# Two buffers for the gate and value rows of an up projection, four instead of five for the left weight parts

## The chip, the cores and the metric

The kernel runs on one core of a Trainium2 chip. The metric is device time in microseconds (us), the median over the runs shown. Times inside the kernel come from one profiled execution.

## What is computed

One decoder layer for 2048 tokens of 1024 features: a mixing block (attention and a recurrent part), and behind it a gated feed-forward block with a causal convolution of width 3. The change is in the feed-forward block:

```python
def conv_gated_ffn(h, w_up, conv_w, conv_b, w_down):
    u = h @ w_up                                   # 1024 -> 2 * 4096
    u_pad = jnp.pad(u, ((0, 0), (CONV_WIDTH - 1, 0), (0, 0)))
    u = conv_b + sum(conv_w[j] * u_pad[:, j:j + S] for j in range(CONV_WIDTH))
    gate, val = jnp.split(u, 2, axis=-1)
    return (jax.nn.gelu(gate, approximate=True) * val) @ w_down

x = x + rms_norm(f, norm_ffn_post[l])              # f: what conv_gated_ffn returns
```

## The kernel before

Phase A projects the input, phase B runs attention, the recurrence and the output projection, and phase D (`phase_d`) is the feed-forward block. All products are float32: each operand is split into a high part (rounded, by a cast on ScalarE, line 40) and a low part (the difference, on VectorE, line 41), and three matmuls replace one (high-high, low-high, high-low).

Both projections of phase D use a Strassen-like scheme with seven products instead of eight. In the up projection the sequence is taken in two halves of 1024 tokens, and in each half there are 32 units; unit n has 128 gate rows and 128 value rows. A unit has seven products j, each of 12 matmuls of 128x512 (line 250) into a bank of PSUM. For each product the weights are combined on GpSimd (lines 218, 219, 224, 227) out of the raw tile `wr`, which two transfers fill (line 205), and split into `wh` and `wl` by `wprep`. The parts of j = 0, 1, 4, 5 come from the left pool, those of j = 2, 3, 6 from the right pool of four buffers. The split activations `hh` and `hl` stay for a whole half.

`product(n, j)` runs the matmuls, and `post(n, j)` what follows. For j = 0, 2, 3 ScalarE copies the bank to `sum` (line 280). For j = 1 a new `ug` tile is taken, two columns of the last half are copied into it (`utile`, line 256), and VectorE adds the `sum` and a bank into its first half (line 276); for j = 4 the second half is added, and `conv` makes the gate: ScalarE does the first tap (line 266), VectorE the other two (lines 267 and 268), and ScalarE the GELU (line 286). For j = 5 a new `uv` tile is taken and its second half added (line 276), and product j = 6 goes on in the same bank `a`; for j = 6 ScalarE copies the bank to `uv` (line 290), the value's convolution follows, and VectorE multiplies gate and value (line 293). Every second unit also writes sums and differences of the results (`sa`, lines 305 to 308), on GpSimd and VectorE. In the first half line 264 keeps two columns of `u` in `halo`.

The units overlap in pairs. In the steady order the slots of seven products are: j=0 of n, j=5 of n-1, j=1 of n, j=4 of n-1, j=2 of n, j=6 of n-1, j=3 of n. `wprep` stands five slots (`LEAD`) ahead of its product in the program. The program's order is the order of priority; the library's planner then orders each engine's instructions by a model of their time, and gives out the buffers of a pool as they come free. Each engine runs its instructions in the planned order. Tiles of a pool that have the same name share the pool's `bufs` buffers.

The down projection takes over the `up_` pool for one constant row (`gpost`).

Of the kernel before, what the change touches and what calls it, by code (L numbers as in the profile page):

```python
# [101 lines left out]
def phase_d(ctx, tc, x1, h2t, w_up, cw, halo, w_down, g_post, mhalf, out, hq, act, td):  # L102
# [8 lines left out]
    with ExitStack() as es:  # L111


        pool = lambda name, bufs=1, side="left": es.enter_context(tc.tile_pool(name=name, bufs=bufs, side=side))
        hrp, wrp, wsp = pool("dr", 2), pool("drw", 2), pool("dsw", 3)
        wps = {"left": pool("dwl", 5)}
        bps = {i: pool(f"d{i}", side="left" if i < 8 else "right") for i in range(14)}
        wps["right"] = pool("dwr", 4, "right")
        up_, ep = pool("du", side="right"), pool("de", side="right")
        pss = [es.enter_context(tc.tile_pool(name=f"dp{i}", bufs=1, space=PSUM)) for i in range(8)]  # L120
        w0c, w1c, w2c, bc = (cw[:, i * 64:(i + 1) * 64] for i in range(4))

# [1042 lines left out]
def hybrid_layer(ctx, tc, a, c, out):  # L1165
# [25 lines left out]
    phase_b(ctx, tc, s, x, a["w_out"][0], a["norm_mix_post"], a["norm_ffn_pre"], a["sinks"], c["tri"], ident, mhalf, gc, line, x1, h2t, hq[0],  # L1191
            cw, a["conv_w"][0], a["conv_b"][0])
    phase_d(ctx, tc, x1, h2t, a["w_ffn_up"][0], cw, halo, a["w_ffn_down"][0], a["norm_ffn_post"],
            mhalf, out[0], hq, act, td)

# [38 lines left out]
```

## Time and profile before

| | |
|---|---|
| median of 3 runs | 3162.61 us (3157.29 to 3166.73) |
| the profiled execution | 3158.45 us, span 3156.6 us |
| TensorE matmul busy | 3043.6 us, 96% of the span |
| TensorE weight load busy | 2458.3 us, 78% |
| VectorE busy | 2302.4 us, 73% |
| ScalarE busy | 1448.5 us, 46% |
| GpSimd busy | 1098.2 us, 35% |

The profile names engines PE (TensorE matmul), PEld (its weight load, which overlaps PE), DVE (VectorE), ACT (ScalarE), POOL (GpSimd) and SP (the queue that issues the transfers). The matmuls are pipelined and their ends are modelled, so the distance of their starts says more than their durations. Idle time stands ahead of the instruction that ended it, with the instruction that released it.

### The profile page before, as it was taken

Reading aid. Unit: us, or ns where it says so; the run is one execution under the profiler, and the core shown is the slowest. Engines: PE = TensorE matmul, PEld = TensorE weight load, DVE = VectorE, ACT = ScalarE, POOL = GpSimd, SP = SyncE. Lnnn points to the kernel's source line nnn. Section 1 sums busy time; section 2 is a strip of 40 time slices with the busy share of each in tenths; the row PEclk is TensorE's granted clock in tenths of the full one; section 3 lists DMA queues with packets and bytes.
Section 4 is the critical chain, followed back from the end, with each engine's and each line's share of the span. In section 5 each row is a group of like instructions: output and inputs, shape, how many; then the busy total and the mean of one; then the engine's idle time right before and its main releaser. Section 6 shows DMA issues by size and latency. Waiting matters only on the chain.

```text
span 3156.6 us, 46475 instructions
## 1 busy us (share of the span) xinstructions
PE 3043.6 (96%) x17897; PEld 2458.3 (78%) x17897; DVE 2302.4 (73%) x3170; ACT 1448.5 (46%) x2438; POOL 1098.2 (35%) x903
## 2 busy tenths in 40 slices
PE   8999999979999998899999999999999999999997
PEld 6788888767777776778787877888887788888786
DVE  6778787766767666999998998888888843334555
ACT  6465756344444445444444445444444432333332
POOL 2212112123323523554444443444444420003642
PEclk9999999969999999999999999999999999999999
DMA  5736363653445635433333343333333474446764
GB/s 162 195 123 187 114 170 104 186 169 108 130 123 161 201 92 196 153 118 101 101 101 101 115 150 123 100 100 100 100 103 101 160 267 151 149 140 227 279 214 167
DMA packets 523762, 461.14 MB, mean 146 GB/s; under 512 B 117306, under 2 KB 405396, under 8 KB 522516
## 3 DMA queue, kind: packets, MB, share of 16 engines
q1 hardware_dynamic: 523540, 458.17, 45.4%
q8 instruction: 140, 2.29, 0.3%
q14 instruction: 82, 0.67, 0.1%
HBM read 316.00 MB, written 142.09 MB: 145 GB/s over the span
## 4 chain that ended last, share of the span: by engine, by line
PE 27%; DVE 18%; DMA 7%; issue 5%; ACT 3%; POOL 0%; SPq 0%; DVEq 0%; POOLq 0%; ACTq 0%
PE b L398 18%; PE b L250 9%; DVE wl L41 7%; DMA wr<-in_w_ffn_up 6%; DVE yg L293 3%; DVE yv L268 2%; ACT yg L266 2%; DVE uv L256 1%; ACT wh L40 1%; DVE ug L276 1%; DVE uv L276 1%; DVE sa L307 0%; DVE sa L306 0%; DVE do L41 0%; DVE yg L267 0%
## 5 line engine op out<-in xcount | busy, mean ns | idle before, releaser
L250 PE MATMUL b<-hh,wh 128*128 128x512 f32 x1792 | 708.9, 396 | 48.0 <-DVE uv L276 33.9
L250 PE MATMUL b<-hh,wl 128*128 128x512 f32 x1792 | 704.8, 394 | 0.5 <-DVE wl L41 0.5
L250 PE MATMUL b<-hl,wh 128*128 128x512 f32 x1792 | 704.7, 393 | 0.2 <-DVE hl L41 0.2
L398 PE MATMUL b<-do 128*128 128x512 f32 x2688 | 613.0, 390 | 5.0 <-DVE do L41 5.0
L398 PEld LDWEIGHTS b<-do 128*128 128x128 f32 x2688 | 506.1, 188 | 111.4 <-DVE do L41 5.9
L41 DVE TENSOR_TENSOR wl<-wr,wh 128x512 fp32r<-128x512 f32 (+1 forms) x400 | 435.1, 1093 | 54.6 <-ACT wh L40 53.3
L250 PEld LDWEIGHTS b<-hh,wh 128*128 128x128 f32 x1792 | 340.3, 190 | 136.7 <-DVE uv L276 47.8
L250 PEld LDWEIGHTS b<-hh,wl 128*128 128x128 f32 x1792 | 339.9, 190 | 74.4 <-DVE wl L41 1.2
L250 PEld LDWEIGHTS b<-hl,wh 128*128 128x128 f32 x1792 | 340.1, 190 | 72.1 <-DVE hl L41 0.6
L41 DVE TENSOR_TENSOR do<-ar,do 128x2048 fp32r<-128x2048 f32 x56 | 138.2, 2467 | 311.4 <-ACT do L40 311.4
L40 ACT CAST wh<-wr 128x512 fp32r<-128x512 f32 (+1 forms) x400 | 274.8, 703 | 172.2 <-PE pj L30 103.5
L218 POOL TENSOR_TENSOR s<-wr 128x512 f32<-128x512 f32 x64 | 131.5, 2054 | 518.1 <-DMA wr<-in_w_ffn_up 518.1
L40 ACT CAST do<-ar 128x2048 fp32r<-128x2048 f32 x56 | 107.1, 1912 | 363.3 <-PE b L398 346.9
L30 PE MATMUL pj<-hh,wh 128*128 128x512 f32 x640 | 256.9, 403 | 4.7 <-ACT hh L40 3.1
L30 PE MATMUL pj<-hh,wl 128*128 128x512 f32 x640 | 255.3, 400 | 0.0
L30 PE MATMUL pj<-hl,wh 128*128 128x512 f32 x640 | 255.0, 400 | 0.0
L161 POOL TENSOR_TENSOR br<-br 128x1024 f32<-128x1024 f32 x32 | 94.9, 2964 | 459.2 <-DMA br<-d_td 358.3
L266 ACT ACTIVATE yg<-ug,cw 128x1024 f32<-128x1024 f32 x64 | 79.7, 1245 | 320.7 <-DVE ug L276 319.0
L40 ACT CAST wh<-s 128x512 fp32r<-128x512 f32 x128 | 79.5, 622 | 189.8 <-POOL s L219 186.4
L30 PEld LDWEIGHTS pj<-hh,wh 128*128 128x128 f32 x640 | 123.0, 192 | 33.3 <-ACT hh L40 3.5
L30 PEld LDWEIGHTS pj<-hl,wh 128*128 128x128 f32 x640 | 122.7, 192 | 26.7
L30 PEld LDWEIGHTS pj<-hh,wl 128*128 128x128 f32 x640 | 122.6, 192 | 26.7
(280 smaller groups left out, 5399.5 us busy)
## 6 DMA issues: line engine op xcount, KB each, us to landing
wr<-in_w_ffn_up SPq DMA_DIRECT2D x128, 512.0 KB
ar<-d_act SPq DMA_DIRECT2D x112, 512.0 KB
br<-in_w_ffn_down SPq DMA_DIRECT2D x72, 512.0 KB
wr<-in_w_in SPq DMA_DIRECT2D x64, 512.0 KB
d_act<-sa SPq DMA_DIRECT2D x32, 1024.0 KB
d_act<-yg SPq DMA_DIRECT2D x32, 512.0 KB
xt<-in_x SPq DMA_DIRECT2D x28, 512.0 KB
d_bk<-bk SPq DMA_DIRECT2D x16, 512.0 KB
```

Of the source, the lines that this page charges most:

```text
L30: nc.tensor.matmul(out=out, lhsT=a, rhs=b, start=first and i == 0 and j == 0, stop=last and i == n - 1 and j == 2)
L40: nc.scalar.copy(out=hi, in_=raw)
L41: nc.vector.tensor_tensor(out=lo, in0=raw, in1=hi, op=ALU.subtract)
L161: nc.gpsimd.tensor_tensor(out=br[:, 0], in0=br[:, 0], in1=br[:, 1], op=ALU.subtract)
L218: tt(out=r[1], in0=t[:, 2], in1=t[:, 3], op=ALU.add)
L250: nc.tensor.matmul(out=o, lhsT=a[:, k, :], rhs=b[:, k, :], start=j in (0, 1, 3) and k == 0 and i == 0, stop=k == 3 and i == 2, skip_group_ ...
L256: nc.vector.tensor_copy(out=u[:, 0:2], in_=halo[:, col, :])
L266: nc.scalar.activation(out=y, in_=u[:, 2:], func=AF.Identity, scale=w2c[:, col:col + 1], bias=bc[:, col:col + 1])
L268: nc.vector.scalar_tensor_tensor(out=y, in0=u[:, 0:SB], scalar=w0c[:, col:col + 1], in1=y, op0=ALU.mult, op1=ALU.add)
L276: nc.vector.tensor_tensor(out=out, in0=x, in1=y, op=ALU.add)
L293: nc.vector.tensor_tensor(out=y, in0=y, in1=yv, op=ALU.mult)
L398: nc.tensor.matmul(out=bks[n], lhsT=x[:, 2 * h + m, a], rhs=b[:, y], start=k == 0 and p not in CHAIN and m == 0 and j == 0, stop=last and ...
```

## The change

The pool of `ug` and `uv` gets two buffers for each of the two tiles. The pool of the left `wh` and `wl` has four of each instead of five.

```diff
         hrp, wrp, wsp = pool("dr", 2), pool("drw", 2), pool("dsw", 3)
-        wps = {"left": pool("dwl", 5)}
+        wps = {"left": pool("dwl", 4)}
         bps = {i: pool(f"d{i}", side="left" if i < 8 else "right") for i in range(14)}
         wps["right"] = pool("dwr", 4, "right")
-        up_, ep = pool("du", side="right"), pool("de", side="right")
+        up_, ep = pool("du", 2, "right"), pool("de", side="right")
```

A left buffer pair takes 2 x 2 KB of each partition, a `ug` or `uv` buffer 4104 bytes.

## Rows read from the trace of the kernel before

**Rows 1.** Line 250's instructions (min/median/max ns); busy us of PE PEld DVE ACT POOL, clock

```profile
L250 PE MATMUL b<-hh,wh x1792: 387/389/794, 1203.4 to 2524.3; 128*128 128x512 f32 x200
1300.00:1400.00 100.00, 88.24 (x364) 70.45 (x363) 88.83 (x92) 39.14 (x60) 54.82 (x32) 0.95 0.41 141
1700.00:1800.00 100.00, 99.06 (x435) 81.06 (x434) 90.78 (x103) 47.23 (x73) 47.33 (x26) 1.00 0.32 106
```

**Rows 2.** Waits of TensorE, 1220 to 2500 us: total us, times, longest

```profile
PE b L250 <- DVE uv L276: 32.6, 32, 4.0
PE b L250 <- ACT sum L280: 5.0, 3, 2.3
```

**Rows 3.** Timeline of TensorE: start us, us, instruction [idle before <-releaser]

```profile
1307.62 0.79 PE L250 MATMUL b<-hh,wh 128*128 128x512 f32 x1 [3.95 <-DVE uv L276]
...
1500.05 0.39 PE L250 MATMUL b<-hh,wh 128*128 128x512 f32 x1
...
1507.98 0.39 PE L250 MATMUL b<-hh,wl 128*128 128x512 f32 x1
...
1531.64 0.50 PE L250 MATMUL b<-hh,wh 128*128 128x512 f32 x1 [0.73 <-DVE uv L276]
...
1958.33 0.50 PE L250 MATMUL b<-hh,wh 128*128 128x512 f32 x1 [3.70 <-DVE uv L276]
```

**Rows 4.** Timeline of VectorE, two units of the steady part

```profile
1489.90 1.25 DVE L256 COPY uv<-halo 128x2 f32<-128x2 f32 x1
...
1514.24 0.68 DVE L276 TENSOR_TENSOR ug<-sum,b 128x512 f32<-128x512 f32 x1
...
1516.23 1.28 DVE L267 SCALAR_TENSOR_TENSOR yg<-ug,cw,yg 128x1024 f32<-128x1024 f32 x1 [0.73 <-ACT yg L266]
...
1519.35 0.17 DVE L256 COPY ug<-halo 128x2 f32<-128x2 f32 x1
1519.43 0.68 DVE L276 TENSOR_TENSOR ug<-sum,b 128x512 f32<-128x512 f32 x1
...
1521.58 1.28 DVE L267 SCALAR_TENSOR_TENSOR yv<-uv,cw,yv 128x1024 f32<-128x1024 f32 x1 [0.87 <-ACT yv L266]
1523.41 0.69 DVE L41 TENSOR_TENSOR wl<-wr,wh 128x512 fp32r<-128x512 f32 x1 [0.55 <-ACT wh L40]
...
1525.21 1.78 DVE L41 TENSOR_TENSOR wl<-wr,wh 128x512 fp32r<-128x512 f32 x1
1526.91 2.31 DVE L293 TENSOR_TENSOR yg<-yg,yv 128x1024 f32<-128x1024 f32 x1
1529.14 1.25 DVE L256 COPY uv<-halo 128x2 f32<-128x2 f32 x1
...
1530.91 0.68 DVE L276 TENSOR_TENSOR uv<-sum,b 128x512 f32<-128x512 f32 x1
...
1533.27 0.67 DVE L276 TENSOR_TENSOR ug<-sum,b 128x512 f32<-128x512 f32 x1
```

**Rows 5.** Chain of work that ended last, 1490 to 1570: start us, us, what

```profile
1518.15 4.59 DMA wr<-in_w_ffn_up
1522.76 0.63 ACT wh L40
```

**Rows 6.** Instructions of lines 276, 293, 256 and 41: ns min/median/max, first and last start

```profile
L276 DVE TENSOR_TENSOR ug<-sum,b x128: 671/677/687, 1224.7 to 2524.9; 128x512 f32<-128x512 f32 x128
L293 DVE TENSOR_TENSOR yg<-yg,yv x64: 1208/2306/2315, 1285.0 to 2532.1; 128x1024 f32<-128x1024 f32 x64
L256 DVE COPY uv<-halo x64: 152/1256/1269, 1221.1 to 2521.3; 128x2 f32<-128x2 f32 x64
L41 DVE TENSOR_TENSOR wl<-s,wh x128: 675/681/1784, 1222.1 to 2493.4; 128x512 fp32r<-128x512 f32 x128
```

**Rows 7.** Timeline of GpSimd in the same stretch

```profile
1528.10 2.27 POOL L224 TENSOR_TENSOR wr<-wr 128x512 f32<-128x512 f32 x1
1532.81 1.69 POOL L227 TENSOR_TENSOR wr<-wr,s 128x512 f32<-128x512 f32 x1 [0.69 <-DVE halo L264]
```

## The prediction

> **What bounds the kernel now.** I read the busy shares by stretch first, since the change touches only the up projection (its matmuls run from 1203.4 to 2524.3 us) and buffers that it uses. In its steady part TensorE is busy 99 per cent at the full granted clock and VectorE 91; near the start TensorE falls to 88 [rows 1]. Second the waits of TensorE in this stage: nearly all of its idle time, 32.6 us in 32 stalls, ends with the add that writes `uv` (L276); no stall of any size waits for a weight part [rows 2]. Third its timeline: matmuls start every 0.2266 us (35 steps from 1500.05 to 1507.98), so the 168 matmuls of two units (a unit is one n, seven products of 12) need 38.07 us. One stall per two units is shown, 0.73 us of idle at 1531.64 [rows 3]; there are 27 of at most 1.5 us on this add, and five larger ones, the first of 3.95 us and the last of 3.70, 14.8 us together, around the start of each half of the sequence [rows 3].
>
> Why there: product j=6 goes into the bank that the add of j=5 still has to read, so TensorE cannot start it before that add. The add sits far back in VectorE's queue. Two units of VectorE, from one `uv` halo copy at 1489.90 to the same copy two units later at 1529.14, take 39.24 us [rows 4], 1.17 us more than TensorE needs. So **the loop that sets the pace is VectorE together with ScalarE**, by 3 per cent, although VectorE is not busy all the time: it waits for ScalarE 0.73 us before the first tap of the gate's convolution, 0.87 us before that of the value's, and in every other unit 0.55 us for a weight cast [rows 4]. The chain of waits tells the same and names one more member: the transfer of the next raw weights (4.59 us), the cast, then the value's taps, and at last the adds [rows 5].
>
> **The change part by part.** The instructions stay the same in number and kind. What changes is which of them may be issued when. The program is ordered by a planner, which lets each engine take the earliest instruction in program order that it takes to be ready; a tile whose buffers are all in use holds back the first instruction that writes it.
>
> *Two `ug` and `uv` buffers.* In the slot order unit n's product j=1 comes before unit n-1's j=4. With one `ug` buffer, the add of j=1 cannot be issued before both taps of unit n-1 have released it: the trace has the halo copy at 1519.35 and the add at 1519.43 right behind the second tap [rows 4]. With two, the add follows its product, ahead of the add of j=4 at 1533.27 [rows 4]. It costs the same wherever it stands, 671 to 687 ns in 128 instances [rows 6], 0.60 us of queue. Its old place was free: from the end of the j=4 add (1514.92) to the value's first tap (1521.58) VectorE follows ScalarE for 6.66 us, and the 0.87 us of idle there merely grows. Its new place is on the path. Alone this is **plus 0.60 us a unit**. The two halo copies of the new buffers wait for the same releases, one unit further ahead, so they stay where they are; the `uv` copy, 1.25 us although its shortest is 0.15 us, ends with GpSimd's operation (1529.14 + 1.25 = 1530.39 against 1528.10 + 2.27 = 1530.37) [rows 4, 7], and I count it unchanged.
>
> *Four left weight buffers.* Products j = 0, 1, 4, 5 use them. Going through the slot order, the cast for a left part can be planned only when the left product four back is done instead of five. In the plan this moves the casts of a unit's four left parts back by a product or two (2.72 us each). On TensorE it should cost nothing: part j=5 of the next unit is written by 1527.0 (1525.21 + 1.78) and used three products after the one that starts at 1531.64, at 1539.8, so 12.8 us ahead [rows 3, 4]; two products later that is still 7.4 us. If that cover goes, each miss costs up to one product, 2.72 us. On VectorE the low parts move with the casts. I worked the order through by hand: part j=0, now between the value's two taps (1523.41, behind 0.55 us of idle), goes behind the multiply L293; part j=5, now ahead of the multiply at 1.78 us (0.68 us where GpSimd is quiet), goes behind the `uv` add; part j=4 goes from ahead of the j=4 add to behind it, where VectorE is idle 0.73 us for ScalarE, and fits (0.60 us of queue) [rows 4].
>
> Sum along the path for an even-odd pair, by those rows: plus 2 x 0.60 for the j=1 adds, minus 2 x 0.60 for part j=4 into the idle time, minus 0.55 for the wait for part j=0, minus 1.1 for one of the two stretched j=5 parts, and plus 0.45 because GpSimd's update L227, 1.69 us and released by part j=1 [rows 7], now falls on the halo copy behind the j=4 add (the copy waits some 1.1 us, the low part adds 0.60, against the 1.31 us between that add's end, 1514.92, and the gate's first tap, 1516.23, that hide them; I count it in one unit of the two). That is **about -1.2 us a pair**, so some 38.0 us, level with TensorE's 38.07. More cannot be had, since TensorE is then the bound. The bounds of the stretched operations are wide: the multiply is 1.21 us at best and 2.31 at most, a low part 0.68 and 1.78 [rows 4, 6], and which of them meets GpSimd is settled by tenths of a microsecond. I take the middle, since GpSimd's bursts start with the same transfer as now.
>
> What the Trainium skill says of this, in "SBUF — State Buffer", section "SBUF: two separate sides": VectorE and GpSimd share one pair of ports as an exclusive lock for a whole instruction, which an operation with two SBUF inputs or a copy in a two-port mode needs. The trace agrees: the low parts, the multiply and the copies are stretched to the end of a GpSimd operation, and the adds, with one input in PSUM, never are [rows 4, 6, 7]. By that rule putting adds beside the GpSimd burst and low parts outside it is a gain, as in my sum; it is no guarantee, for the same lock can catch other operations.
>
> What it is worth: the 27 small stalls are 32.6 - 14.8 = 17.8 us of shown idle; the shown idle understates a stall by about 0.16 us (at 1531.64 the loss by start times is 0.89, shown 0.73), so 17.8 + 27 x 0.16 = 22 us. I expect nine tenths of it, 20 us, and 2 of the 14.8 us in the larger stalls, whose order is another one at the start of each half. Together 22 us. The other stages stay: the down projection follows with TensorE as its bound and moves up by the same amount.
>
> The profiled execution took 3158.45 us (span 3156.6), 4 us below the median 3162.61 of the three runs, whose spread is 9.4. **Forecast: 3158.45 - 22 = 3136.5 us.**
>
> **The rivals.**
> *The adds move, the weight parts do not (slower).* If the plan keeps the low parts where they are, only the first term is left: the j=1 add comes onto the path and its old place turns into idle time before the value's taps. From the first pair on VectorE's loop is up to 0.60 us a unit longer, and TensorE already follows it: at most 64 x 0.60 = 38 us, 3197 us; with half of the units caught 19 us, 3177. For it: the path has no slack, 39.24 against 38.07. Against it: the same release rule that frees `ug` also holds the left parts, and the present order has them at their first possible place.
> *It changes little.* Work moved equals work moved: one add against one low part a unit, and which operations meet GpSimd's decides the rest; the loop stays at 39.2, or the `uv` add was never held by its buffer. Time 3158, plus or minus 9. For it: no instruction goes away.
> *All stalls on `uv` go.* If the large ones go as well: 22 + 14.8 = 37 us, and 5.0 us of the waits for the `sum` copy and some matmuls at the lower granted clock in their wake: some 3115 us.
>
> **How the numbers follow.** Forecast (-12 to -30) 0.42, all stalls 0.12, little 0.20, slower 0.26. About 0.3 per cent, 9.5 us, can be told from no change. Faster 0.54, same 0.18, slower 0.28, the edges of the cases being shared out. The range for 8 in 10 reaches from the case without stalls, 3112, to the slower one with nearly all units caught, 3188; the forecast's own is 3128 to 3146.
>
> **What would show it.** In the trace of the changed kernel: the `ug` add of j=1 ahead of the j=4 add and not behind the gate's second tap; a low part in the idle time before the gate's first tap; the distance of equal `uv` copies two units apart near 38.1 instead of 39.24 us; waits of TensorE for L276 well under 32.6 us. Wrong would be: that distance at 40 us or more with the idle time before the value's taps at 1.5 us (the slower rival), stalls of TensorE for L40 or L41 (the cover of the weights gone), or an order of VectorE that is the same but for a few copies.

## The result and the profile after

The change takes the kernel from 3164.67 to 3130.1 us in runs side by side, a ratio of 0.9893 (95% interval 0.9872 to 0.9913). The profiled execution took 3131.27 us (span 3129.5), against 3158.45 (3156.6) before; these two lie 27 us apart and not 35, since the one before is among the shorter of its executions and the one of the changed kernel among the longer.

The up projection alone became 35.6 us shorter in the profiled executions: its matmuls ran from 1203.4 to 2524.3 us [rows 1] and now run from 1208.0 to 2493.3. It starts 4.6 us later, which is not the change: the planned order ahead of it is the same, and a second execution of the changed kernel started it at 1204.6. Behind it 3.9 us are lost, on which more below. The rows that answer to [rows 1], line 250 with its first and last start, and the busy time by stretch (us, then busy us and count of PE, PEld, DVE, ACT and POOL, the granted clock, the DMA share and GB/s):

```profile
L250 PE MATMUL b<-hh,wh x1792: 387/389/796, 1208.0 to 2493.3; 128*128 128x512 f32 x200
...
1300.00:1400.00 100.00, 92.00 (x385) 74.03 (x386) 92.35 (x99) 44.12 (x67) 58.94 (x34) 0.97 0.46 156
1700.00:1800.00 100.00, 99.69 (x436) 81.11 (x435) 90.34 (x106) 49.23 (x75) 41.57 (x26) 1.00 0.35 113
```

In both stretches TensorE is busier than before; VectorE's busy share is the same in the steady part and higher near the start. No work went away. The waits of TensorE in the stage, which answer to [rows 2] (us in total, times, longest):

```profile
PE b L250 <- DVE uv L276: 12.8, 7, 3.6
PE b L250 <- ACT wh L40: 4.1, 1, 4.1
PE b L250 <- ACT sum L280: 3.9, 5, 1.4
```

Of 32 stalls on the `uv` add 7 are left, of 32.6 us 12.8. Five are large ones at the starts of the halves, two are small, as the timeline of TensorE shows, beside [rows 3]:

```profile
1301.02 0.50 PE L250 MATMUL b<-hh,wh 128*128 128x512 f32 x1 [2.45 <-DVE uv L276]
...
1347.68 0.79 PE L250 MATMUL b<-hh,wh 128*128 128x512 f32 x1 [3.58 <-DVE uv L276]
...
1793.78 0.50 PE L250 MATMUL b<-hh,wh 128*128 128x512 f32 x1 [0.31 <-DVE uv L276]
...
1918.14 0.79 PE L250 MATMUL b<-hh,wh 128*128 128x512 f32 x1 [3.17 <-DVE uv L276]
```

The timeline of VectorE, one unit of the steady part, beside [rows 4]. In brackets behind an instruction is the idle time ahead of it:

```profile
1506.94 0.68 DVE L276 TENSOR_TENSOR ug<-sum,b 128x512 f32<-128x512 f32 x1
1507.54 1.46 DVE L41 TENSOR_TENSOR wl<-wr,wh 128x512 fp32r<-128x512 f32 x1
1508.93 0.16 DVE L264 COPY halo<-ug 128x2 f32<-128x2 f32 x1
1509.00 1.27 DVE L267 SCALAR_TENSOR_TENSOR yg<-ug,cw,yg 128x1024 f32<-128x1024 f32 x1
...
1514.33 1.28 DVE L267 SCALAR_TENSOR_TENSOR yv<-uv,cw,yv 128x1024 f32<-128x1024 f32 x1 [1.45 <-ACT yv L266]
1515.65 1.28 DVE L268 SCALAR_TENSOR_TENSOR yv<-uv,cw,yv 128x1024 f32<-128x1024 f32 x1
1516.85 1.77 DVE L41 TENSOR_TENSOR wl<-wr,wh 128x512 fp32r<-128x512 f32 x1
1518.55 2.31 DVE L293 TENSOR_TENSOR yg<-yg,yv 128x1024 f32<-128x1024 f32 x1
1520.78 1.26 DVE L256 COPY uv<-halo 128x2 f32<-128x2 f32 x1
...
1522.55 0.67 DVE L276 TENSOR_TENSOR uv<-sum,b 128x512 f32<-128x512 f32 x1
1523.15 1.18 DVE L41 TENSOR_TENSOR wl<-wr,wh 128x512 fp32r<-128x512 f32 x1
...
1524.32 0.68 DVE L276 TENSOR_TENSOR ug<-sum,b 128x512 f32<-128x512 f32 x1
1524.92 0.68 DVE L41 TENSOR_TENSOR wl<-wr,wh 128x512 fp32r<-128x512 f32 x1
1525.52 0.68 DVE L276 TENSOR_TENSOR ug<-sum,b 128x512 f32<-128x512 f32 x1
```

The two `ug` adds now follow each other (1524.32 is j=1 of the next unit, 1525.52 j=4 of this one), the low part of j=4 (1507.54) fills the time in which VectorE waited for ScalarE ahead of the gate's tap, and the wait ahead of the value's tap has grown from 0.87 to 1.45 us.

The measure for the steady part is the distance of two units: from the first matmul of product j=0 of one unit to that of the unit two further on, found by counting 12 matmuls to a product along line 250. I give the mean of 11 such distances in the first half (units 8 to 28) and of 12 in the second (units 38 to 60).

| kernel | time, us | before, beside it | ratio, 95% interval | first half | second half |
|---|---|---|---|---|---|
| before | | | | 39.30 | 39.08 |
| the change | 3130.1 | 3164.67 | 0.9893 (0.9872 to 0.9913) | 38.56 | 38.26 |
| left4 | 3125.96 | 3162.82 | 0.9881 (0.9866 to 0.9895) | 38.21 | 38.21 |
| ug2_left5 | 3196.64 | 3162.82 | 1.011 (1.0095 to 1.0125) | 40.79 | 40.53 |
| uv2_left5 | 3155.18 | 3162.82 | 0.9978 (0.9968 to 0.9988) | 39.26 | 38.99 |
| ug2_left4 | 3131.41 | 3162.82 | 0.9904 (0.9887 to 0.992) | 38.49 | 38.40 |
| ug2_j4own | 3158.21 | 3160.88 | 0.9988 (0.9978 to 0.9998) | 39.38 | 39.12 |
| j4own | 3135.34 | 3160.88 | 0.9916 (0.9902 to 0.9931) | 38.41 | 38.27 |
| left3 | 3207.4 | 3160.88 | 1.0149 (1.0132 to 1.0167) | 40.98 | 41.08 |
| left4_b | 3124.46 | 3164.5 | 0.9873 (0.9858 to 0.9887) | 38.21 | 38.21 |
| after_b | 3130.35 | 3164.5 | 0.9889 (0.9874 to 0.9904) | 38.44 | 38.34 |
| left4_haloact | 3123.29 | 3164.5 | 0.9871 (0.9854 to 0.9887) | 38.21 | 38.21 |

No such distance in any kernel is below 38.21 us, and in left4 all of them are 38.21 and the profile shows TensorE's matmuls busy without a gap (420.30 of the 420.30 us from 1401.6 to 1821.9). So I take 38.21 us as TensorE's own time for 168 matmuls.

### The profile page after: what moved, and what is told of

Read it like the earlier page. It is cut to its first block, busy times and chain, and to the rows that moved or that the text cites. A ratio compares the mean times of both kernels' runs of the same rounds, so it can differ in the third digit from the quotient of the medians.

```text
span 3129.5 us, 46406 instructions
## 1 busy us (share of the span) xinstructions
PE 3034.0 (97%) x17897; PEld 2455.5 (78%) x17897; DVE 2313.7 (74%) x3170; ACT 1448.6 (46%) x2438; POOL 1034.2 (33%) x903
## 4 chain that ended last, share of the span: by engine, by line
PE 63%; DVE 20%; issue 6%; ACT 4%; DMA 3%; POOL 2%; SPq 1%; DVEq 0%; POOLq 0%; ACTq 0%
PE b L398 17%; PE b L250 14%; PE pj L30 14%; DVE wl L41 6%; PE m L30 5%; PE pp L895 2%; DVE yg L293 2%; DVE yg L268 1%; DVE yv L267 1%; DVE ug L276 1%; DVE yg L267 1%; ACT yv L266 1%; PE po L1062 1%; ACT yg L286 1%; PE lo L587 1%
## 5 line engine op out<-in xcount | busy, mean ns | idle before, releaser
L250 PE MATMUL b<-hh,wh 128*128 128x512 f32 x1792 | 705.9, 394 | 22.0 <-DVE uv L276 12.8
L41 DVE TENSOR_TENSOR wl<-wr,wh 128x512 fp32r<-128x512 f32 (+1 forms) x400 | 458.2, 1147 | 38.6 <-ACT wh L40 37.4
L218 POOL TENSOR_TENSOR s<-wr 128x512 f32<-128x512 f32 x64 | 101.4, 1584 | 461.5 <-DMA wr<-in_w_ffn_up 461.5
L267 DVE SCALAR_TENSOR_TENSOR yv<-uv,cw,yv 128x1024 f32<-128x1024 f32 x64 | 83.8, 1309 | 82.9 <-ACT yv L266 82.9
```

Of the source, the lines that this page charges most:

```text
L41: nc.vector.tensor_tensor(out=lo, in0=raw, in1=hi, op=ALU.subtract)
L218: tt(out=r[1], in0=t[:, 2], in1=t[:, 3], op=ALU.add)
L250: nc.tensor.matmul(out=o, lhsT=a[:, k, :], rhs=b[:, k, :], start=j in (0, 1, 3) and k == 0 and i == 0, stop=k == 3 and i == 2, skip_group_ ...
L267: nc.vector.scalar_tensor_tensor(out=y, in0=u[:, 1:SB + 1], scalar=w1c[:, col:col + 1], in1=y, op0=ALU.mult, op1=ALU.add)
```

## The experiments

**Which half of the change gives the gain.** The four kernels below take the change apart. Where one of the tiles `ug` and `uv` has two buffers, the other keeps one; the row `gpost`, which takes over a `ug` buffer later, then names the same count (left out of the cuts below).

left4, the left pool alone:

```diff
-        wps = {"left": pool("dwl", 5)}
+        wps = {"left": pool("dwl", 4)}
```

> Four left weight buffers, ug and uv with one buffer as before. Theory (the later weight parts give the gain, and the second ug buffer takes part of it back, because its add leaves idle time for the path): 3118 to 3132 us, as fast as the whole change or a little faster; equal products two units apart at 38.2 us in both halves of the sequence (39.2 before). Rival 1 (the gain comes from the second buffers of ug and uv): 3157 to 3170, as before. Rival 2 (it takes both): between, 3140 to 3157.

Measured 3125.96 us, 38.21 us for two units in both halves: the theory. The timeline of VectorE, here in the first half, shows why there is no second price: the add of j=1 (1534.39) still lies behind the gate's second tap, ahead of the same 0.87 us of idle as before, and the part of j=4 (1529.75) has moved behind the j=4 add:

```profile
1529.15 0.67 DVE L276 TENSOR_TENSOR ug<-sum,b 128x512 f32<-128x512 f32 x1
1529.75 1.47 DVE L41 TENSOR_TENSOR wl<-wr,wh 128x512 fp32r<-128x512 f32 x1
1531.14 0.15 DVE L264 COPY halo<-ug 128x2 f32<-128x2 f32 x1
1531.21 1.27 DVE L267 SCALAR_TENSOR_TENSOR yg<-ug,cw,yg 128x1024 f32<-128x1024 f32 x1
...
1534.39 0.68 DVE L276 TENSOR_TENSOR ug<-sum,b 128x512 f32<-128x512 f32 x1
1534.98 0.68 DVE L41 TENSOR_TENSOR wl<-s,wh 128x512 fp32r<-128x512 f32 x1
1536.54 1.29 DVE L267 SCALAR_TENSOR_TENSOR yv<-uv,cw,yv 128x1024 f32<-128x1024 f32 x1 [0.87 <-ACT yv L266]
```

ug2_left5, two buffers for `ug` alone, the left pool of five:

```diff
-                u = up_.tile([P, SB + 2], F32, name="ug" if b == 0 else "uv")
+                u = up_.tile([P, SB + 2], F32, name="ug" if b == 0 else "uv", bufs=2 if b == 0 else 1)
```

> Two ug buffers, one uv buffer, five left weight buffers. Theory: the j=1 add stands on the path and nothing is moved into its old place, so up to 0.60 us a unit: 3178 to 3203 us, two units 40.4 us apart, 1.4 us idle before the value's second tap. Rival 1 (the buffers give the gain): 3125 to 3145.

Measured 3196.64 us, 34 us slower than before, and 1.48 and 1.45 us more for two units (from unrounded means), where 1.20 had been worked out. TensorE's waits for the `uv` add double, and the timeline of VectorE has the add of j=1 (1539.21) ahead of that of j=4, 1.46 us of idle ahead of the value's tap, and the wait for a cast behind it:

```profile
PE b L250 <- DVE uv L276: 63.8, 58, 4.2
```

```profile
1528.04 1.28 DVE L267 SCALAR_TENSOR_TENSOR yv<-uv,cw,yv 128x1024 f32<-128x1024 f32 x1 [1.46 <-ACT yv L266]
1529.95 0.69 DVE L41 TENSOR_TENSOR wl<-wr,wh 128x512 fp32r<-128x512 f32 x1 [0.63 <-ACT wh L40]
...
1539.21 0.67 DVE L276 TENSOR_TENSOR ug<-sum,b 128x512 f32<-128x512 f32 x1
1539.81 1.40 DVE L41 TENSOR_TENSOR wl<-wr,wh 128x512 fp32r<-128x512 f32 x1
1541.13 0.67 DVE L276 TENSOR_TENSOR ug<-sum,b 128x512 f32<-128x512 f32 x1
```

So the second `ug` buffer, alone, is the slower rival of the prediction. Two buffers for both tiles with five left ones were not run; by the next kernel the second `uv` buffer should add nothing.

uv2_left5, two buffers for `uv` alone:

```diff
-                u = up_.tile([P, SB + 2], F32, name="ug" if b == 0 else "uv")
+                u = up_.tile([P, SB + 2], F32, name="ug" if b == 0 else "uv", bufs=1 if b == 0 else 2)
```

> Two uv buffers, one ug buffer, five left weight buffers. Theory: the uv halo copy keeps its place for one unit further ahead, so nothing changes: 3157 to 3170 us, 39.2 us for two units, waits for the uv add as before (32 us). Rival 1 (the buffer of uv holds the add that TensorE waits for): 3125 to 3145, waits for the uv add under 15 us.

Measured 3155.18 us, a little below the expected band. In the steady part the order of VectorE's instructions is that of before and the distances hardly change (39.26 and 38.99 us for two units), and the waits on the `uv` add are those of before:

```profile
PE b L250 <- DVE uv L276: 32.6, 28, 4.2
```

The buffer of the tile whose add TensorE waits for is thus not what holds it. The kernel is 0.2 per cent faster all the same, which the interval tells from no change; most of that is outside the steady part and was not followed up.

ug2_left4, the change without the second `uv` buffer:

> The change without the second uv buffer. Theory: as the whole change, 3125 to 3135 us. Rival 1 in its form that uv's buffer is what counts: 3150 or more.

Measured 3131.41 us, as expected. The order of VectorE's instructions is that of the change, but for the halo copy into `uv`, which is for the next unit instead of the one after it.

**Which of the moved parts.** The left pool of four moves the low parts of all four left products by one place: that of j=0 to behind the value's taps, that of j=5 to behind the `uv` add, that of j=1 from there to behind the part of j=5, and that of j=4 to behind the j=4 add. A buffer of its own for j=4, with four for the other three kinds, holds back the part of j=4 alone, since the next unit's part of j=4 then has to wait for this unit's product:

```diff
-        wps = {"left": pool("dwl", 5)}
+        wps = {"left": pool("dwl", 4)}
...
-                hi = wp.tile([P, 4, P], F32R, name="wh")
-                lo = wp.tile([P, 4, P], F32R, name="wl")
+                hi = wp.tile([P, 4, P], F32R, name="wh", tag="wh4" if j == 4 else "wh", bufs=1 if j == 4 else 4)
+                lo = wp.tile([P, 4, P], F32R, name="wl", tag="wl4" if j == 4 else "wl", bufs=1 if j == 4 else 4)
```

ug2_j4own has this beside two `ug` buffers, where TensorE's own pace does not cut the gain off:

> Two ug buffers as in the slow kernel; of the left weight parts that of j=4 alone is held back, by a buffer of its own (the other three kinds share four). In the program only the low part of j=4 moves, from ahead of the j=4 add into the idle time behind it. Theory (the moved parts act one by one; this one is worth 0.60 us a unit where GpSimd's update does not catch it, 0.4 where it does): two units 39.3 to 39.9 us apart against 40.7, 3157 to 3174 us. Rival A (the gain is in parts j=0 and j=5, which leave the way of the value's taps): 3188 to 3200. Rival B (part j=4 is all of it): 3126 to 3140.

Measured 39.38 and 39.12 us for two units, 1.4 us less than without the hold, and 3158.21 us: the theory, neither of the two rivals. The add of j=1 and the low part of j=4 have changed places, and the two balance. The timeline shows the three instructions and, behind them, the halo copy that GpSimd holds up (1.26 us):

```profile
1511.67 1.28 DVE L276 TENSOR_TENSOR ug<-sum,b 128x512 f32<-128x512 f32 x2
1512.86 0.68 DVE L41 TENSOR_TENSOR wl<-wr,wh 128x512 fp32r<-128x512 f32 x1
1513.46 1.26 DVE L264 COPY halo<-ug 128x2 f32<-128x2 f32 x1
1514.64 1.27 DVE L267 SCALAR_TENSOR_TENSOR yg<-ug,cw,yg 128x1024 f32<-128x1024 f32 x1
```

j4own has it with one buffer for `ug` and `uv`:

> The same hold on part j=4 with one buffer for ug and uv each, as before. Theory: 39.2 minus 0.75 to 1.2, so 38.2 to 38.5 us for two units, 3126 to 3145 us. Rival A: 3155 to 3168, 39.2 us.

Measured 3135.34 us, 38.41 and 38.27 us: this one moved instruction gives 25.5 us. A rival would be that the gain comes from GpSimd, whose busy time for two units the change lowers from 18.7 to 16.3 us; but here it is 18.3 and 18.2 us, hardly less than before. With two `ug` buffers the other moved parts together give the rest: from 39.38 and 39.12 (ug2_j4own) to 38.49 and 38.40 us (ug2_left4). They were not moved one by one.

**How far the parts can be held back.** left3 has a left pool of three:

```diff
-        wps = {"left": pool("dwl", 5)}
+        wps = {"left": pool("dwl", 3)}
```

> Three left weight buffers, ug and uv with one. The casts move back by one more left product. Theory (the weights are written far enough ahead; TensorE is already the bound with four): 38.2 us for two units, 3118 to 3132 us. Rival (the cover of the weights is gone): TensorE waits for lines 40 and 41 in the steady part, 3140 us or more.

Measured 3207.4 us, 47 slower than before. The theory fell and the rival came, though not by the casts' lateness alone. The waits of TensorE, and the timelines of the queue that issues the transfers, of ScalarE and of VectorE:

```profile
PE b L250 <- DVE wl L41: 60.4, 57, 2.9
```

```profile
1533.95 1.00 SPq L205 DMA_DIRECT2D wr<-in_w_ffn_up  x2
```

```profile
1538.63 1.66 ACT L40 CAST wh<-wr 128x512 fp32r<-128x512 f32 x3 [6.48 <-DMA wr<-in_w_ffn_up]
```

```profile
1533.24 0.69 DVE L41 TENSOR_TENSOR wl<-wr,wh 128x512 fp32r<-128x512 f32 x1
...
1539.29 1.29 DVE L41 TENSOR_TENSOR wl<-wr,wh 128x512 fp32r<-128x512 f32 x2 [2.83 <-ACT wh L40]
```

The low part of j=4 now comes behind the value's taps (1533.24), later than that of j=6, and it reads the raw weights last; their buffer is released only then, and the next transfer starts at 1533.95, behind the value's taps, where before it started behind the part of j=6 between the gate's taps (1518.15 in [rows 5]). ScalarE and VectorE then wait for the transfer, 6.48 and 2.83 us. I had followed the lead of the casts before their products and not who releases the raw weights.

**What the second buffers cost in the whole change.** The kernel with four left buffers alone and the whole change, side by side:

> Four left weight buffers with one buffer for ug and uv, side by side with the whole change, to tell whether the second buffers cost anything. Theory: 38.21 us for two units in both halves of the sequence, against 38.56 in the first half for the whole change (14 pairs, so some 4 to 5 us): 3120 to 3128 us. Rival (no difference): both within 2 us of each other.

> The whole change again, beside it. Theory: 3127 to 3133 us, 3 to 6 us above the kernel with four left buffers alone. Rival: no difference.

Measured 3124.46 us (four runs, 3123.74 to 3125.27) and 3130.35 us (3125.8 to 3131.88). The ranges don't overlap, the intervals of the two ratios do; two units take 38.21 us in the one and 38.44 and 38.34 in the other. So the second buffers cost some 5 us here, but not in one place. In the profiled executions of this pair, and of the change and left4, the way from the first matmul of the up projection to the end of the kernel is 4.6 and 4.2 us longer with them:

| where, us longer with the second buffers | after_b less left4_b | the change less left4 |
|---|---|---|
| first eight units | -4.1 | -8.5 |
| the two steady parts | 4.0 | 4.4 |
| the crossing between the halves (units 30 to 38) | 1.6 | 2.8 |
| the last two units | 0.6 | 0.7 |
| behind the up projection | 2.5 | 4.8 |

So, beside four left buffers, the second buffers make the start faster and the rest slower; ug2_left4 against left4 shows the same signs, so it is the one for `ug` that does it. left4 is the better version of the two.

left4_haloact, the same with the halo copies of line 256 on ScalarE:

```diff
-                nc.vector.tensor_copy(out=u[:, 0:2], in_=halo[:, col, :])
+                nc.scalar.copy(out=u[:, 0:2], in_=halo[:, col, :])
```

> Four left weight buffers, one ug and uv, and the two copies of halo columns into ug and uv on ScalarE instead of VectorE (1.25 us of VectorE's queue for the one into uv). Theory (TensorE is already the bound in the steady part; only the start and the crossing between the halves can gain): 38.2 us for two units, 3112 to 3128 us. Rival (VectorE's queue is still the bound): under 3110 us.

Measured 3123.29 us, not to be told from left4_b, and 38.21 us again, as the theory has it. But the edit relieved VectorE of little: the wait for GpSimd that stretched the copy now falls for the most part on the low part behind it, and VectorE's busy time in the two steady parts went from 812.3 (left4_b) to 805.5 us only, 0.3 us for two units. That TensorE is the bound there is shown by its matmuls without a gap, and this run agrees with it.

## Why the prediction was right, and where its sizes were off

*What bounds the kernel.* Right: VectorE's loop with ScalarE, not its busy time. VectorE's busy share in the steady part is the same before and after (90.78 and 90.34 of 100 us), and the loop still came down to nearly TensorE's time. In the second half (units 38 to 62) its busy time even rose from 410.02 to 421.16 us for the same 24 units, in a stretch that became 9.9 us shorter (columns as above, before and after):

```profile
2002.80:2471.80 469.00, 462.23 (x2017) 377.50 (x2016) 410.02 (x433) 221.03 (x337) 224.49 (x120) 1.00 0.31 101
```

```profile
1983.70:2442.80 459.10, 459.10 (x2018) 378.32 (x2017) 421.16 (x431) 220.99 (x334) 196.25 (x120) 1.00 0.32 103
```

The floor was put at 38.07 us; it is 38.21.

*The add of j=1 comes onto the path.* Right in sign and place, shown by ug2_left5; its size was 0.72 to 0.74 us a unit instead of 0.60. The idle time ahead of the value's tap was expected to grow, and did, by 0.58 to 0.59 us.

*The halo copies stay where they are.* Right: the `uv` copy stands behind the multiply in both kernels and takes 1.25 and 1.26 us; uv2_left5 shows the steady part unmoved by a second `uv` buffer.

*The low parts move.* Two of three are where they were put: that of j=4 fills the idle time ahead of the gate's tap, and that of j=5 stands behind the `uv` add (1523.15). The third, j=0, has left the place between the value's taps, and with it the wait of 0.55 us, but it stands ahead of the multiply (1516.85) and not behind it, and is stretched to 1.77 us there by GpSimd as that of j=5 was [rows 4]. So the saving of 1.1 us for j=5 did not come as written: part j=5 is shorter now (1.18 us) and part j=0 longer. All low parts together, by the sum of their durations, take 14.3 and 14.4 us for two units in the two steady parts, against 13.3 before: GpSimd stretches them more than it did, and the gain is in the idle time that they fill. GpSimd's update L227 does fall behind the j=4 add, but it costs 0.07 us there and not 0.45: it holds up the part of j=4 (1.46 us), the halo copy has moved behind that part (1508.93), and the tap starts at 1509.00 against 1506.94 + 0.68 + 1.31 = 1508.93. All of this was worked out on units of the first half; in the second line 264 does not run, so that copy and its term do not exist there.

*The sum.* -1.2 us for two units was expected, level with TensorE's time. Measured are -0.74 and -0.83, where the floor of 38.21 us would have allowed -1.09 and -0.87. The runs give the terms: 1.48 and 1.45 us for the j=1 adds (ug2_left5) instead of 1.20, -1.41 in both halves for the part of j=4 (ug2_j4own) instead of -1.20, and -0.89 and -0.72 for the other parts (ug2_left4), which the floor may cut short, instead of -0.55 - 1.1 + 0.45 = -1.20. The errors cancel in part. By 11 and 12 distances the measured gain is 8.1 + 9.9 = 18 us in the steady part, against the 20 expected. The term that was mis-sized is the one for the starts of the halves. The five larger stalls on the `uv` add went from 14.8 to 2.45 + 1.91 + 3.58 + 1.20 + 3.17 = 12.3 us, close to the 2 us expected. But the first eight units became 9.2 us shorter (195.6 to 186.4) and the eight at the crossing between the halves 6.3 us (171.4 to 165.1). By the distances of matmul starts in these two stretches, some 8.6 of these 15.5 us are stalls of over 0.6 us, for the copies to `sum` too, and 6.4 us are matmuls that start 0.3 to 0.6 us after the one before, 63 now instead of 97; the granted clock of the first stretch rose from 0.93 to 0.96. The last two units make up the 2 us that remain. The busy time by stretch of that first part, before and after (columns as above):

```profile
1203.40:1402.00 198.60, 175.62 (x721) 139.98 (x718) 166.13 (x167) 90.76 (x139) 99.52 (x64) 0.93 0.46 155
```

```profile
1208.00:1400.00 192.00, 174.19 (x729) 139.73 (x730) 163.78 (x173) 95.03 (x143) 102.15 (x64) 0.96 0.49 165
```

I had counted the stalls on one releaser and left out the others in the same stretch and the slower matmuls behind them. The runs also tell the two stretches apart. The first eight units become much shorter only where both edits are together (188.4 us in after_b, 186.8 in ug2_left4, but 194.9 and 192.5 with four left buffers alone and 195.6 in ug2_left5); why was not followed up. The crossing gains by the left buffers alone (162.3 us in left4).

The time came out closer than the difference. 22 us were forecast, 27.2 lie between the two profiled executions and 34.6 between the medians; that the sum started from the profiled execution, 4 us under the median, hid part of that, which is luck.

*The other stages move up by the same amount.* Not quite. At the border to the down projection the wait for the second set of operands ends later in relation to the last matmul of the stage: 2556.28 - 2524.3 = 32.0 us before, 2528.28 - 2493.3 = 35.0 us after. The two starts, in the timelines of TensorE of the kernel before and of the changed one:

```profile
2556.28 3.93 PE L398 MATMUL b<-do 128*128 128x512 f32 x16 [1.14 <-DVE do L41]
```

```profile
2528.28 21.93 PE L398 MATMUL b<-do 128*128 128x512 f32 x89 [1.36 <-DVE do L41]
```

and the chain of waits of the changed kernel ahead of it, in the main two transfers and GpSimd's work between them (the difference of line 161 and the last one of line 308), with short waits for the queue of transfers left out:

```profile
2498.88 7.27 DMA br<-in_w_ffn_down
2506.31 3.90 POOL br L161
2510.21 2.24 POOL sa L308
...
2515.93 7.99 DMA ar<-d_act
```

This chain starts with VectorE's work on the last units and not with TensorE. With one `ug` buffer and four left ones the same distance is 31.2 and 31.4 us (left4, left4_b), with two `ug` buffers and four left ones 34.4 (ug2_left4, after_b): the loss comes with the second `ug` buffer. That it comes by this chain is read from the trace and was not tried alone; the other 0.9 us of the 3.9 were not followed up.

*The rivals.* The slower one is real, and is what the second `ug` buffer does without the smaller left pool: 34 us, within the 19 to 38 given to it. What spoke against it (the same release rule holds the left parts) is what decided. The cover of the weights held at four buffers: the low parts caused no stall in the changed kernel's steady part. At three it is gone, by a chain that the prediction had not looked at.

## What to carry to other kernels

When two in-order engines wait for each other in a loop, look at which instruction stands in the idle time that the loop cannot avoid: here moving one there was worth at least its whole time, and taking one out cost as much, with no instruction added or removed. Buffer counts set the planned order, so a buffer less can be faster because it holds something back from the path; test each count alone, for here one of two edits gave 37 us by itself, and the other cost 34 without it and 5 to 6 with it. Before a count is lowered further, look up who reads a loaded tile last, since that sets the start of the next transfer.

## What the runs showed of the hardware

Nothing that was unexpected in kind. In size: an add that is moved onto the path cost 0.72 to 0.74 us a unit where its own time in the queue is 0.60, and the low parts took anything from 0.68 to 1.78 us, by where GpSimd's operations fell; a sum made with one duration for them can only be right on average. And taking away an instruction that GpSimd's operation stretches did not free its time: in left4_haloact the stretch passed for the most part to the next low part, and of the copies of 1.25 us a unit only 0.3 us for two units came free.
